# Retention scores taken two rounds earlier, in the preceding token tile's last attention unit

## The chip, the cores and the metric

The kernel runs on one core of one Trainium2 chip. The metric is the device time of one execution in microseconds (us), the median of several runs. The engines are named as in the profile: PE (TensorE, matrix products; PEld its weight loads), DVE (VectorE), ACT (ScalarE), POOL (GpSimd) and SP (SyncE, which here issues the DMAs). Each engine works through its own instructions in the order in which the program lists them, and waits at an instruction until the semaphores named there have been reached.

## What is computed

Two layers of a streaming encoder over 2048 tokens of width 1024. Each layer normalises its input, projects it by `w_in` to eight sections, runs two groups of heads side by side, gates them and projects back by `w_out`:

```python
def hybrid_layer(x, norm_gain, w_in, w_out, rel_bias, cos, sin):
    hn = rms_norm(x, norm_gain)
    aq, ak, av, ag, rq, rk, rv, rg = jnp.split(hn @ w_in, cuts, axis=-1)
    ya = chunked_rel_attention(aq, ak, av, rel_bias)
    yr = chunkwise_retention(rq, rk, rv, cos, sin)
    y = jnp.concatenate([ya * silu(ag), yr * silu(rg)], axis=-1)
    return x + y @ w_out
```

The attention (8 heads of 64) sees a chunk of 64 tokens and the 8 chunks before it. The change concerns the other half, the retention (4 heads of 128). In its chunkwise form, with rotated q and k:

```python
    att = jnp.einsum("bnihd,bnjhd->bnhij", qc, kc) * intra_decay[None, None]
    o_intra = jnp.einsum("bnhij,bnjhe->bnihe", att, vc)
    kv = jnp.einsum("bnjhd,hj,bnjhe->bnhde", kc, k_decay, vc)
    # state is carried over the chunks: state = state * chunk_decay + kv
    o_inter = jnp.einsum("bnihd,hi,bnhde->bnihe", qc, q_decay, states)
    o = rms_norm(o_intra + o_inter)
```

## The kernel before

**Tiling.** The kernel loops over layers l, four head groups s (two attention heads and one retention head each), and four token blocks n of 512 tokens. A block has four token tiles a of 128 tokens; t = 4n + a. All large products are done in two or three terms of f16 halves, so that they keep f32's accuracy: a value is split in an upper half (ACT) and a rest (DVE).

**Rounds.** The order of the instructions of PE, ACT, DVE and POOL is written by hand (`manual_schedule`); only SP's order is left to a scheduler. `run` (L1140) steps through the dense projections of a block: `dense_T` (L608, transposed sections q, k, rotated rq and rk; 12 steps) and `dense_V` (L738, token-major sections v, rv and gates; 12 steps). A step is 8 matmuls of 128x512, a third of one dense product, and is called a round here. After each step, `run` first calls `tick` (L598), which issues the pieces that were put off by `later(k, ...)` (L595) k rounds ago, then takes one step of the attention of the *preceding* block, then pulls some background work (weight preparation, for the first pass also the tables and the normalisation of later tokens, `norms_from_input`, L1154).

**Attention.** `attention` (L778) has 8 units per block, three rounds each: unit (a, hx) for head hx of token tile a. In its first round a unit finishes an older unit's product with v (`flow`, then `pv`, L815, which reads the transposed probabilities pT at L820 to L822) and takes its own scores (`qk`, L785: PE at L800 and L801 into the PSUM tile S, then bias and maximum on DVE at L804, exponential on ACT at L807, halves on ACT and POOL at L809 and L810, and one round later a DMA transpose to pT at L812). Of the two units of a token tile, the one with hx = 0 is called even and the other odd.

**Retention.** The generator `retention` (L866) has two steps per token tile. The first takes the scores r1 (three matmuls of rotated halves, at L856 in the helper `products`), and puts off the multiplication with the decay mask (DVE, L875) by one round, the upper half of dT (ACT, `upper_of`, L860) by two, its rest (DVE, `rest_of`, L864) by three. The second step takes r2: dT with rv, the rotated q with the state's halves sh, and the products of the token-major keys kt with rv for the state; the state's update follows put off in the same way (L896, and `upper_of` and `rest_of` again for sh), and so do the sum of squares, the root on POOL and the gated result (L908 to L913). All four r and o tiles at a time share the PSUM pool `psR` (4 banks); dT is a single buffer.

Counted in rounds from a token tile's first, the scores are taken in round 0, just behind the even unit's attention scores, and r2 in round 5:

```python
            u = qk(a, hx)
            if i % 2 == 0 and not slow:
                next(ret, None)
            yield
            yield
            if i % 2 == 1 or slow:
                next(ret, None)
```

In the first block of all (`slow`) the scores are taken two rounds later, in round 2.

**The rotated keys.** In `dense_T`, `swap` (L664) turns the section's product with the tables in steps put off over several rounds. For rk the low half (`lower`, L676, DVE) is issued in round 19 of the block's 24, and the transpose kt to token-major form (`tokens`, L683, a DMA on SP's queue) in round 23.

Of the kernel before, what the change touches and what calls it, by code (L numbers as in the profile page):

```python
# [18 lines left out]
P = 128  # L19
# [8 lines left out]
def hybrid_trunk(ctx: ExitStack, tc: tile.TileContext, x, pos, gain, gcol, w_in, w_out, rel, fgain,  # L28
# [746 lines left out]
            yield  # L775


    def attention(l, s, n, g, st, prev):  # L778
        units = []
        for a in range(4):  # L780
            for hx in range(2):
                units.append((a, hx))
        ya = {}

        def qk(a, hx):  # L785

            u = St()
            u.a, u.hx = a, hx
            u.nm = f"{l}_{s}_{n}_{a}_{hx}"
            u.nb = nb = min(5, 4 * n + a + 1)  # L790
            u.w = w = nb * P
            u.kts = [(st if t // 4 == n else prev, t % 4) for t in range(4 * n + a + 1 - nb, 4 * n + a + 1)]
            S = psS.tile([P, 1024], F32, tag="S", name=f"S{u.nm}")
            cs = slice(a * P, (a + 1) * P)
            cuts = sorted({0, nb} | {j for j in range(nb) if u.kts[j] == (st, 0) or j == 4})
            for j0, j1 in zip(cuts, cuts[1:]):
                q_, a_ = u.kts[j0]
                k_ = q_.k[:, hx, a_ * P:(a_ + j1 - j0) * P]
                o = S[:, j0 * P:j1 * P]
                pe.matmul(o, st.q[:, hx, 0, cs], k_, start=True, stop=False)  # L800
                pe.matmul(o, st.q[:, hx, 1, cs], k_, start=False, stop=True)  # L801
            v = b2.tile([P, 640], F32, tag="sc", name=f"sc{u.nm}")[:, 0:w]
            m = b2.tile([P, 1], F32, tag="mq", name=f"mq{u.nm}")
            dve.tensor_tensor_reduce(out=v, in0=S[:, 0:w], in1=g.bias[hx][:, 640 - w:640], scale=1.0, scalar=-3.0e38,  # L804
                                     op0=ALU.add, op1=ALU.max, accum_out=m)
            dve.tensor_scalar(m, m, g.nc[:, 0:1], LN_PSC, op0=ALU.mult, op1=ALU.add)  # L806
            act.activation(v, v, AF.Exp, bias=m[:, 0:1], scale=g.c[:, 0:1])  # L807
            pq = b2.tile([P, 1280], F16, tag="pq", name=f"pq{u.nm}")
            act.activation(pq[:, 0:w], v, AF.Copy)  # L809
            pool.tensor_tensor(pq[:, w:2 * w], v, pq[:, 0:w], op=ALU.subtract)  # L810
            u.p = b2.tile([P, 10, P], F16, tag="pT", name=f"pT{u.nm}")[:, 0:2 * nb, :]
            later(1, lambda: sp.dma_start_transpose(out=u.p, in_=pq[:, 0:2 * w]))  # L812
            return u

        def pv(u):  # L815
            t = 4 * n + u.a
            o = psR.tile([P, 512], F32, tag="small", name=f"o{u.nm}")
            for b, (q_, a_) in enumerate(u.kts):
                v_ = q_.v[:, a_, u.hx, :]
                pe.matmul(o[:, 0:65], u.p[:, b, :], v_[:, 0:65], start=(b == 0), stop=False)  # L820
                pe.matmul(o[:, 0:64], u.p[:, b, :], v_[:, 65:129], start=False, stop=False)  # L821
                pe.matmul(o[:, 0:65], u.p[:, u.nb + b, :], v_[:, 0:65], start=False, stop=(b == u.nb - 1))  # L822

            def out_():
                rl = b2.tile([P, 1], F32, tag="rl", name=f"rl{u.nm}")
                dve.reciprocal(rl, o[:, 64:65])
                dve.tensor_tensor(rl, rl, g.ka, op=ALU.mult)
                if u.hx == 0:
                    ya[u.a] = b2.tile([P, P], F32, tag="ya", name=f"ya{u.nm}")
                y = ya[u.a]  # L830
                vs = slice(u.hx * 64, u.hx * 64 + 64)
                dve.scalar_tensor_tensor(out=y[:, vs], in0=o[:, 0:64], scalar=rl[:, 0:1], in1=st.g[u.a][:, vs],
                                         op0=ALU.mult, op1=ALU.mult)
                if u.hx == 1:
                    sp.dma_start(y_d[t][:, s * P:(s + 1) * P], y)

            later(1, out_)

        ret = retention(l, s, n, g, st)
        slow = (l, s, n) == (0, 0, 0)  # L840
        for i, (a, hx) in enumerate(units):
            flow(1)
            u = qk(a, hx)
            if i % 2 == 0 and not slow:
                next(ret, None)
            yield
            yield
            if i % 2 == 1 or slow:
                next(ret, None)
            pipe.append(lambda u=u: pv(u))  # L850
            yield


    def products(out_, pairs):
        for i, (w_, m_) in enumerate(pairs):
            pe.matmul(out_, w_, m_, start=(i == 0), stop=(i + 1 == len(pairs)))  # L856
# [5 lines left out]
    def rest_of(dst, src):  # L862

        dve.scalar_tensor_tensor(out=dst[:, 1], in0=dst[:, 0], scalar=-2.0 ** 11, in1=src, op0=ALU.mult, op1=ALU.add)  # L864

    def retention(l, s, n, g, st):  # L866
        for a in range(4):
            t = 4 * n + a
            nm = f"{l}_{s}_{t}"
            cs = slice(a * P, (a + 1) * P)  # L870
            last = t == NT - 1
            r1 = psR.tile([P, 512], F32, tag="small", name=f"r1{nm}")
            products(r1[:, 0:P], [(st.rk[:, i, cs], st.rq[:, j, cs]) for i, j in ((0, 0), (0, 1), (1, 0))])
            dT = b1.tile([P, 2, P], F16, tag="dT", name=f"dT{nm}")
            later(1, lambda r1=r1: dve.tensor_tensor(r1[:, P:2 * P], r1[:, 0:P], g.msk, op=ALU.mult))  # L875
            later(2, lambda dT=dT, r1=r1: upper_of(dT, r1[:, P:2 * P]))
            later(3, lambda dT=dT, r1=r1: rest_of(dT, r1[:, P:2 * P]))
            yield
            r2 = psR.tile([P, 512], F32, tag="small", name=f"r2{nm}")
            rv = st.rv[a]  # L880
            terms = [(dT[:, 0], rv[:, 0]), (dT[:, 0], rv[:, 1])]
# [477 lines left out]
    for l in range(DEPTH):  # L1359
        gO = [Grp(), Grp()]  # L1360
        go = Grp()
        for s in range(NSW):
            g = grp(l, s)
            for n in range(NS):
                first = (l, s, n) == (0, 0, 0)
                if not first:
                    st = St()
                    states[l, s, n] = st
                    dT = dense_T(l, s, n, g, st)
                else:  # L1370
                    st = st0
                if n == 0 and not first:
                    bs, bt = bias_scratch(l, s), bias_tiles(l, s, g)
                    later(1, lambda bs=bs: next(bs))
                    for k in (4, 8, 17, 21):
                        later(k, lambda bt=bt: next(bt))
                if (l, s) == (0, 0) and 0 < n < NS - 1:
                    if n == 1:
                        push(t1, TAB_STEPS - 10)
                    push(norms_from_input(range(4 * n + 4, 4 * n + 8), late[0:4] if n == 1 else None,  # L1380
                                          tables(n + 1, [xs0[n + 1][:, i * 256:(i + 1) * 256] for i in range(4)])), 21)
                if (l, s, n) == (0, 1, 1):
                    for l_ in range(1, DEPTH):
                        gr = gain_scale(l_)
                        later(2, lambda gr=gr: next(gr))
                        later(10, lambda gr=gr: next(gr))
                        later(18, lambda gr=gr: next(gr))
                if n == (NS - 1 if (l, s) == (0, 0) else 1):
                    if s + 1 < NSW:
                        push(prep_T(l, s + 1, grp(l, s + 1)), 25)  # L1390
                    else:
                        push(prep_O(l, 0, gO[0], go), 9)
                if n == NS - 1 and s == 1 and l + 1 < DEPTH:
                    gain_load(l + 1)
                if not first:
                    run(dT, att, 10 if n == 0 else 14 if (l, s, n) == (0, 0, NS - 1) else 22 if (l, s) == (0, 0) else 24)
                if n == NS - 1 and s == NSW - 1:
                    us = []
                    push(wout_first(l, go, us), 10)
                if n == 2 and s == 2:  # L1400
                    push(prep_Omax(l, go), 13)
                if n == NS - 1:
                    if s + 1 < NSW:
                        push(prep_V(l, s + 1, grp(l, s + 1)), 23)
                    else:
                        push(prep_O(l, 1, gO[1], go), 9)
                run(dense_V(l, s, n, g, st), att, 24 if n == NS - 1 and s < NSW - 1 else 12)
                if first:
                    sp_order.__exit__(None, None, None)
                if att[0] is not None:  # L1410
                    drain(att[0])
                att = [attention(l, s, n, g, st, states.get((l, s, n - 1)))]
        pull(1000)
        if l + 1 == DEPTH:
            ring["fg"] = b3.tile([P, D], F32, tag="wh", name="fg")
# [81 lines left out]
```

## Time and profile before

| | |
|---|---|
| median of 3 runs | 2116.13 us (2115.45 to 2116.34) |
| span of the profiled execution | 2120.7 us, 4.6 us above that median |
| PE busy | 95% of the span |
| DVE busy | 63% |
| ACT busy | 54% |
| POOL busy | 20% |

The profile is of one execution. A time of a row is in us from the start of the span, durations of single instructions in ns where the row says min/median/max. In a table of waits a row reads: engine, what it writes, line, then what ended the wait, then the total, how often and the longest. A line such as L856 is that of a helper, so the names of the tiles tell the use: `r<-rot,rot` are the retention's scores, `r<-rv,dT` the products that read them. In the slices of the page the first two of 40 (the start-up) show the lowest share of PE, 0.6 and 0.7; after them it is 0.8 or more in each.

### The profile page before, as it was taken

To read this page: it belongs to the slowest core of one execution; us is meant where nothing else is said; L and a number is where in the kernel's file an instruction comes from. 1 tells how busy PE (TensorE), PEld (TensorE's weight loads), DVE (VectorE), ACT (ScalarE), POOL (GpSimd) and SP (SyncE) were. 2 spreads that over 40 slices of the span, in tenths; PEclk is the share of its full clock that TensorE was granted. 3 is DMA by queue.
4 is the path that set the end of the run, shared out by engine and by line. 5 is a ranking of instruction groups with operands and counts; after the bars stand their busy time and mean duration, and the time that the engine had idled before them with its cause. 6 is when DMAs were issued, how large, how long until landed. Compare 5 with 4: busy or idle time off the path is not lost.

```text
span 2120.7 us, 39351 instructions
## 1 busy us (share of the span) xinstructions
PE 2014.2 (95%) x14014; PEld 1052.9 (50%) x14014; DVE 1341.8 (63%) x4031; ACT 1136.9 (54%) x2522; POOL 432.8 (20%) x509
## 2 busy tenths in 40 slices
PE   6788999999999999988999999999999999998998
PEld 4334455555555555444444555555555555554543
DVE  7667666666656666566654666566666566666643
ACT  7455565556565554554544546554655665445432
POOL 1112221222122212221000222222222222222200
PEclk9989999999999999999999999999999999999999
DMA  8757675557476765689865556655666866648864
GB/s 247 173 111 162 138 157 119 115 110 156 109 166 133 157 164 100 120 189 254 219 179 123 119 100 135 130 119 100 140 129 123 172 152 157 124 101 176 217 193 127
DMA packets 645702, 313.63 MB, mean 148 GB/s; under 512 B 459233, under 2 KB 602081, under 8 KB 645505
## 3 DMA queue, kind: packets, MB, share of 16 engines
q1 hardware_dynamic: 645504, 311.12, 66.4%
q8 instruction: 109, 1.79, 0.4%
q14 instruction: 89, 0.72, 0.1%
HBM read 123.26 MB, written 41.98 MB: 78 GB/s over the span
## 4 chain that ended last, share of the span: by engine, by line
PE 50%; DMA 8%; DVE 5%; ACT 5%; issue 1%; SPq 1%; POOL 0%; POOLq 0%; DVEq 0%; ACTq 0%
PE dT L731 16%; PE dV L752 15%; PE dO L1093 12%; DMA pT<-pq 3%; PE r L856 2%; PE S L800 2%; PE S L801 2%; DVE sc L804 1%; DMA toep<-rel_d 1%; DMA swp<-rot 1%; PE o L820 1%; ACT pq L809 1%; PE o L821 1%; PE o L822 1%; ACT sc L807 1%
## 5 line engine op out<-in xcount | busy, mean ns | idle before, releaser
L807 ACT ACTIVATE sc<-sc,mq,cT 128x640 f32<-128x640 f32 (+4 forms) x256 | 218.4, 853 | 657.3 <-DVE mq L806 341.5
L810 POOL TENSOR_TENSOR pq<-sc,pq 128x640 f16<-128x640 f32 (+4 forms) x256 | 322.6, 1260 | 1201.7 <-ACT pq L809 610.3
L731 PE MATMUL dT<-hTh,whT 128*128 128x512 f16 x1008 | 350.2, 383 | 13.4 <-DMA hTh<-hTl 9.8
L752 PE MATMUL dV<-whV,hTh 128*128 128x512 f16 x1024 | 355.3, 383 | 4.1 <-DVE gt L770 4.1
L752 PE MATMUL dV<-wlV,hTh 128*128 128x512 f16 x1024 | 353.8, 381 | 0.0
L752 PE MATMUL dV<-whV,hTl 128*128 128x512 f16 x1024 | 353.7, 381 | 0.0
L731 PE MATMUL dT<-hTh,wlT 128*128 128x512 f16 x1008 | 347.0, 379 | 0.0
L731 PE MATMUL dT<-hTl,whT 128*128 128x512 f16 x1008 | 346.8, 379 | 0.0
L752 PEld LDWEIGHTS <-hTh 128*128 128x128 f16 x2048 | 197.5, 99 | 222.9 <-issue 8.2
L731 PEld LDWEIGHTS <-whT 128*128 128x128 f16 x2016 | 192.9, 98 | 225.8 <-issue 23.1
L804 DVE CUSTOM_DVE_ANT_0 sc<-S,bias 128x640 f32<-128x640 f32 (+4 forms) x256 | 188.6, 737 | 79.9 <-PE S L801 69.0
L1093 PE MATMUL dO<-whO,yhy 128*128 128x512 f16 x512 | 195.0, 381 | 1.1 <-DMA yhy<-rhy 1.1
L1093 PE MATMUL dO<-whO,yly 128*128 128x512 f16 x512 | 194.8, 381 | 1.1 <-DMA yly<-rly 1.1
L1093 PE MATMUL dO<-wlO,yhy 128*128 128x512 f16 x512 | 194.6, 380 | 0.0
L809 ACT ACTIVATE pq<-sc 128x640 f16<-128x640 f32 (+4 forms) x256 | 171.5, 670 | 12.5 <-DMA pT<-pq 4.6
L1093 PEld LDWEIGHTS <-yhy 128*128 128x128 f16 x1024 | 100.0, 98 | 116.7 <-DMA yhy<-rhy 1.9
L752 PEld LDWEIGHTS <-hTl 128*128 128x128 f16 x1024 | 99.5, 98 | 110.5 <-issue 2.6
L731 PEld LDWEIGHTS <-wlT 128*128 128x128 f16 x1008 | 97.6, 98 | 109.0 <-issue 1.8
L800 PE MATMUL S<-k,q 128*128 128x128 f16 (+3 forms) x592 | 143.7, 269 | 5.7 <-DVE mq L804 5.6
L820 PE MATMUL o<-v,pT 128*128 128x65 f16 x1120 | 130.2, 194 | 14.6 <-DMA pT<-pq 14.6
L820 PEld LDWEIGHTS <-pT 128*128 128x128 f16 x1120 | 105.6, 97 | 52.5 <-DMA pT<-pq 24.4
L801 PE MATMUL S<-k,q 128*128 128x128 f16 (+3 forms) x592 | 131.2, 270 | 0.0
(350 smaller groups left out, 3354.4 us busy)
## 6 DMA issues: line engine op xcount, KB each, us to landing
q<-qq SPq DMA_DIRECT2D x128, 128.0 KB, 2.5
yyy<-y_d SPq DMA_DIRECT2D x32, 512.0 KB, 4.6
stT<-in_w_in_dram SPq DMA_DIRECT2D x27, 512.0 KB, 5.0
stV<-in_w_in_dram SPq DMA_DIRECT2D x26, 512.0 KB, 4.5
k<-kk SPq DMA_DIRECT2D x128, 64.0 KB, 2.1
swp<-rot SPq DMA_DIRECT2D x64, 128.0 KB, 2.6
tabc<-tab SPq DMA_DIRECT2D x32, 256.0 KB, 2.7
tabs<-tab SPq DMA_DIRECT2D x32, 256.0 KB, 2.8
```

Of the source, the lines that this page charges most:

```text
L731: pe.matmul(ps, w_[:, j, kt, :], h_[:, kt, :], start=(m == 0), stop=(m == 23))
L752: pe.matmul(ps, h_[:, kt, a * P:(a + 1) * P], w_[:, kt, :], start=(m == 0), stop=(m == 23))
L800: pe.matmul(o, st.q[:, hx, 0, cs], k_, start=True, stop=False)
L801: pe.matmul(o, st.q[:, hx, 1, cs], k_, start=False, stop=True)
L804: dve.tensor_tensor_reduce(out=v, in0=S[:, 0:w], in1=g.bias[hx][:, 640 - w:640], scale=1.0, scalar=-3.0e38, op0=ALU.add, op1=ALU.max, accu ...
L807: act.activation(v, v, AF.Exp, bias=m[:, 0:1], scale=g.c[:, 0:1])
L809: act.activation(pq[:, 0:w], v, AF.Copy)
L810: pool.tensor_tensor(pq[:, w:2 * w], v, pq[:, 0:w], op=ALU.subtract)
L820: pe.matmul(o[:, 0:65], u.p[:, b, :], v_[:, 0:65], start=(b == 0), stop=False)
L821: pe.matmul(o[:, 0:64], u.p[:, b, :], v_[:, 65:129], start=False, stop=False)
L856: pe.matmul(out_, w_, m_, start=(i == 0), stop=(i + 1 == len(pairs)))
L1093: pe.matmul(ps, h_[:, kt, :], w_[:, kt, :], start=(m == 0), stop=(m == 23))
```

## The change

The scores of a token tile move out of `retention` into a function of their own, `decayed`. In the odd unit of token tile a, one round after its attention scores, `attention` now calls `decayed` for token tile a + 1; in the last unit of a block for the first token tile of the next block (`nxt`), whose state object is therefore made earlier. Counted from the token tile's first round the scores so stand in round -2, mask, upper half and rest in rounds -1, 0 and 1. `retention` keeps the second step, r2, in round 5. The first block of all takes its first tile's scores in round 2 as before. The first block of the second layer, which has no attention ahead of it, takes them by a `later(11, ...)` in its own dense steps.

```diff
+            yield
+            if hx == 1:
+                if a < 3:
+                    decayed(l, s, n, g, st, a + 1)
+                elif nxt is not None:
+                    decayed(*nxt, 0)
+            yield
+            if hx == 1:
                 next(ret, None)
-            yield
-            yield
-            if i % 2 == 1 or slow:
-                next(ret, None)
+            elif a == 0 and (l, s, n) == (0, 0, 0):
+                decayed(l, s, n, g, st, 0)
...
+    def decayed(l, s, n, g, st, a):
+        nm = f"{l}_{s}_{4 * n + a}"
+        cs = slice(a * P, (a + 1) * P)
+        r1 = psR.tile([P, 512], F32, tag="small", name=f"r1{nm}")
+        products(r1[:, 0:P], [(st.rk[:, i, cs], st.rq[:, j, cs]) for i, j in ((0, 0), (0, 1), (1, 0))])
+
+        def upper():
+            st.dT = b1.tile([P, 2, P], F16, tag="dT", name=f"dT{nm}")
+            upper_of(st.dT, r1[:, P:2 * P])
+
+        later(1, lambda: dve.tensor_tensor(r1[:, P:2 * P], r1[:, 0:P], g.msk, op=ALU.mult))
+        later(2, upper)
+        later(3, lambda: rest_of(st.dT, r1[:, P:2 * P]))
...
-            r1 = psR.tile([P, 512], F32, tag="small", name=f"r1{nm}")
-            products(r1[:, 0:P], [(st.rk[:, i, cs], st.rq[:, j, cs]) for i, j in ((0, 0), (0, 1), (1, 0))])
-            dT = b1.tile([P, 2, P], F16, tag="dT", name=f"dT{nm}")
-            later(1, lambda r1=r1: dve.tensor_tensor(r1[:, P:2 * P], r1[:, 0:P], g.msk, op=ALU.mult))
-            later(2, lambda dT=dT, r1=r1: upper_of(dT, r1[:, P:2 * P]))
-            later(3, lambda dT=dT, r1=r1: rest_of(dT, r1[:, P:2 * P]))
-            yield
+            dT = st.dT
...
+                if (n, s) == (0, 0) and not first:
+                    later(11, lambda n=n, g=g, st=st: decayed(l, s, n, g, st, 0))
```

The instructions of each engine stay the same in number. In the built programs' order, PE's score products, DVE's masks and rests and ACT's upper halves of dT move. In SP's queue, which a scheduler orders, some twenty DMAs change places with a neighbour; among them the transpose kt of the second block, which now stands ahead of the last lower rows hTl of the third block's normalised tokens, and the loads of the next decay mask.

More of the change, by code (lines that the diff above doesn't have):

```diff
@@ L775, in dense_V, with attention @@
             yield
-    def attention(l, s, n, g, st, prev):
+    def attention(l, s, n, g, st, prev, nxt):
         units = []
@@ L839, in attention @@
         ret = retention(l, s, n, g, st)
-        slow = (l, s, n) == (0, 0, 0)
         for i, (a, hx) in enumerate(units):
@@ L843, in attention @@
             u = qk(a, hx)
-            if i % 2 == 0 and not slow:
+            yield
[6 more added lines that the diff above has]
+            if hx == 1:
                 next(ret, None)
-            yield
-            yield
-            if i % 2 == 1 or slow:
-                next(ret, None)
+            elif a == 0 and (l, s, n) == (0, 0, 0):
+                decayed(l, s, n, g, st, 0)
             pipe.append(lambda u=u: pv(u))
@@ L1366, in hybrid_trunk @@
                 if not first:
-                    st = St()
-                    states[l, s, n] = st
+                    st = states.setdefault((l, s, n), St())
                     dT = dense_T(l, s, n, g, st)
@@ L1411, in hybrid_trunk @@
                     drain(att[0])
-                att = [attention(l, s, n, g, st, states.get((l, s, n - 1)))]
+                m = n + 1 if n + 1 < NS else 0
+                nxt = (l, s + (m == 0), m)
+                if nxt[1] < NSW:
+                    nxt += (grp(*nxt[:2]), states.setdefault(nxt, St()))
+                else:
+                    nxt = None
+                att = [attention(l, s, n, g, st, states.get((l, s, n - 1)), nxt)]
         pull(1000)
```

## Prediction

> **What bounds the kernel now.** I read the page first, then the table of who waited for whom, cut by engine and by window, then the timeline at the places that it points to.
>
> ```profile
> span 2120.7 us, 39351 instructions
> PE 2014.2 (95%) x14014; PEld 1052.9 (50%) x14014; DVE 1341.8 (63%) x4031; ACT 1136.9 (54%) x2522; POOL 432.8 (20%) x509
> ```
>
> TensorE (PE) is busy for 95% of the span, so a change that leaves its instructions alone can only win idle time of PE: 2120.7 - 2014.2 = 106.5 us. The sums below are made in this profiled execution, whose span is 4.6 us (0.2%) above the median of the runs, 2116.1 us. I carry the difference over to the median.
>
> What PE waited for stands in the table of waits (total us, times, longest):
>
> ```profile
> PE r L856 <- DVE dT L864: 20.5, 16, 5.1
> PE o L820 <- DMA pT<-pq: 14.6, 13, 2.4
> PE r L856 <- ACT dT L860: 10.2, 6, 2.9
> ...
> PE r L856 <- DVE sh L864: 2.9, 3, 1.7
> ```
>
> The largest item of PE's idle time is the one that the change goes for. The products at L856 that read dT (the decayed scores in two halves, upper from ACT, rest from DVE) wait 20.5 + 10.2 = 30.7 us in 22 places. That is 1.4% of the span, and the ceiling of what dT alone can give back. The other rows matter too: the attention's transposed probabilities pT (14.6 us) and the state's halves sh (2.9 us) come through the same engines, and are what PE would meet next.
>
> **The change part by part.** Nothing is added or removed. Per token tile one mask product, one upper half and one rest move (127 of the 128 of each, in the order of instructions of the built programs), with the three matmuls ahead of them:
>
> ```profile
> L856 PE MATMUL r<-rot,rot x384: 219/219/314, 85.8 to 1977.5; 128*128 128x128 f16 x192
> L875 DVE TENSOR_TENSOR r<-r,msk x128: 286/290/300, 87.9 to 1980.7; 128x128 f32<-128x128 f32 x128
> L860 ACT ACTIVATE dT<-r x128: 253/259/277, 90.7 to 1983.4; 128x128 f16<-128x128 f32 x128
> L864 DVE SCALAR_TENSOR_TENSOR dT<-dT,r x128: 272/278/289, 91.0 to 1985.2; 128x128 f16<-128x128 f16 x128
> ```
>
> Before, with 6 rounds to a token tile, the scores stand in round 0, mask in 1, upper in 2, rest in 3, the reading products in 5. After, they stand in rounds -2, -1, 0, 1, and the products still in 5. PE's work is the same: the three matmuls stood behind the attention scores and now stand alone behind a third of a dense product; I cost that at nothing, between -0.1 us and +0.1 us per token tile (half of the 219 ns of one matmul), and take the middle. PSUM: the built program gives each r1 the bank of the r1 before it, read last by rest, three rounds earlier; no new wait there unless DVE is more than three rounds late.
>
> So dT's slack grows from two rounds to four. Its longest wait is 5.1 us, in the first layer's first pass, where the old order of the very first tile left no slack at all. I expect the dT waits to go. The question is what is late next. I split the 30.7 us by place.
>
> *First pass, 85 to 215 us.* The waits of PE in this window:
>
> ```profile
> PE r L856 <- DVE dT L864: 9.9, 4, 5.1
> PE r L856 <- ACT dT L860: 6.6, 4, 2.9
> PE dT L731 <- DMA hTh<-rhn: 3.6, 1, 3.6
> ```
>
> 16.5 us of dT waits are here. But here DVE and ACT also normalise the next tiles' tokens, and the dense products of a tile (L731) begin when the transposed rows hTh have landed. The second tile's start at 145.24 us and the SP queue and landing of its last rows:
>
> ```profile
> 140.41 2.08 SPq L236 DMA_TRANSPOSE hTh<-rhn  x1
> ...
> DMA to landing us min/median/max: 4.1/4.1/4.1
> ...
> 145.24 1.89 PE L731 MATMUL dT<-hTh,whT 128*128 128x512 f16 x8
> ```
>
> hTh lands at 140.41 + 4.1 = 144.5 us, 0.7 us before PE uses it; at the next such start, 210 us, PE waits for it already (3.6 us above). PE can gain only what the DVE and ACT work ahead of those transposes gains. How much of that work waits for PE?
>
> ```profile
> DVE sc L804 <- PE S L801: 5.1, 3, 3.0
> ```
>
> Only 5.1 us, the longest right behind the 5.1 us stall of PE. Against it stands a move in SP's queue: in the built order the transpose kt of the second tile now stands ahead of the last lower rows hTl, and it waits for products of PE. One such issue costs 1.2 to 1.3 us:
>
> ```profile
> L683 SPq DMA_TRANSPOSE kt<-rot x32: 1231/1349/2368, 85.9 to 1934.7; - x32
> ```
>
> Bounds for this part: -1.3 us (nothing caught up, the transpose in the way) to +16.5 us. I take 5.1 - 1.2 = **3.9 us**, since the hTh row says that PE is held to the DVE chain.
>
> *The rest of the run.* The dT waits from 215 to 960 us, and from 960 us on:
>
> ```profile
> PE r L856 <- DVE dT L864: 6.3, 7, 1.7
> PE r L856 <- ACT dT L860: 1.8, 1, 1.8
> ...
> PE r L856 <- DVE dT L864: 4.3, 5, 1.5
> PE r L856 <- ACT dT L860: 1.8, 1, 1.8
> ```
>
> 14.2 us. Of these 2.6 + 1.0 = 3.6 stand where each layer ends (870 to 980 and 1900 to 1990 us), and there PE waits for pT right behind them:
>
> ```profile
> PE o L820 <- DMA pT<-pq: 5.6, 4, 2.1
> ...
> PE r L856 <- DVE dT L864: 2.6, 2, 1.7
> ...
> PE o L820 <- DMA pT<-pq: 1.2, 2, 0.9
> PE r L856 <- DVE dT L864: 1.0, 1, 1.0
> ```
>
> I count those 3.6 as lost to pT. The other 10.6 us hold two twin places (636 and 1667 us, 2.2 us each). There the new position of the scores meets a wait of its own. They read the low half of the rotated keys, which DVE finishes in the stretch below; PE would stand at the new place at 632.3, where the next dense matmul now starts:
>
> ```profile
> 632.28 0.38 PE L752 MATMUL dV<-whV,hTl 128*128 128x512 f16 x1
> ...
> 632.68 0.68 DVE L676 TENSOR_TENSOR rot<-raw,rot 128x512 f16<-128x512 f32 x1
> ...
> 635.93 0.28 PE L856 MATMUL r<-rv,dT 128*128 128x128 f16 x2 [1.76 <-ACT dT L860]
> ```
>
> The scores wait 632.68 + 0.68 - 632.28 = 1.1 us, half of the 2.2 us that were won. So these two places keep 1.1 us each of 2.2, and 10.6 - 2.2 = 8.4 us remain. Of a won stall, PE keeps as much as the next pT has in hand. An example, the stall of 1.51 us at 730.65:
>
> ```profile
> 730.65 0.23 PE L856 MATMUL r<-rv,dT 128*128 128x128 f16 x1 [1.51 <-DVE dT L864]
> ...
> 734.93 1.34 SPq L812 DMA_TRANSPOSE pT<-pq  x1
> ...
> DMA to landing us min/median/max: 3.4/3.4/3.4
> ...
> 738.97 0.19 PE L820 MATMUL o<-v,pT 128*128 128x65 f16 x1
> ```
>
> pT lands at 734.93 + 3.4 = 738.3, used at 738.97: 0.7 us in hand, so 0.7 of 1.51 is kept, 44%. With that share: 8.4 x 0.44 = **3.7 us** (between 0 and 14.2).
>
> *Displacement.* Mask and upper now stand ahead of the next even unit's bias-and-maximum (DVE) and exponential (ACT), which they stood behind. The odd units have the same work ahead of them as before. Each of 128 even units can lose up to 0.29 + 0.26 = 0.55 us of pT's time. PE's weight loads waited for pT 22 times; ACT waited for DVE ahead of the exponential 145 times in 256:
>
> ```profile
> PEld L820 <- DMA pT<-pq: 24.4, 22, 2.9
> ...
> ACT sc L807 <- DVE mq L806: 341.5, 145, 5.9
> ```
>
> So upper mostly hides in ACT's idle time, and mask costs only where DVE is behind and the unit even. About 11 of the 22 waits would be of even units; a third of them at 0.29 us makes **1.0 us** lost (bounds 0 and 22 x 0.55 = 12.1 us).
>
> Sum: 3.9 + 3.7 - 1.0 = 6.6 us. 2116.1 - 6.6 = **2109.5 us**.
>
> *The clock.* After the 5.07 us stall PE is slow:
>
> ```profile
> 110.43 0.29 PE L856 MATMUL r<-rv,dT 128*128 128x128 f16 x1 [5.07 <-DVE dT L864]
> ...
> 110.83 3.12 PE L752 MATMUL dV<-whV,hTh 128*128 128x512 f16 x8
> ...
> 85.00:145.00 60.00, 47.51 (x264) 22.71 (x263) 40.71 (x116) 33.11 (x71) 10.44 (x15) 0.89 0.59 118
> 145.00:211.00 66.00, 55.92 (x408) 29.32 (x406) 46.84 (x129) 36.85 (x78) 16.30 (x18) 0.96 0.71 152
> ```
>
> Eight matmuls take 3.12 us there and 1.89 us at 145.24, 1.23 us more. At granted clocks of 0.89 and 0.96 the two windows lose up to 47.5 x 0.11 + 55.9 x 0.04 = 7.4 us of PE time. I add nothing for it, since PE is not what sets the end of these windows; it belongs to the first rival.
>
> The Trainium skill, "TensorE: Matmul & The Clock Gate", Part 1, says that PE runs at half rate after an idle window of about 3.4 us and until it has been busy for as long. The rows above agree. The rule speaks against the change at one point: if the short dT stalls of the first pass are gathered into one longer wait for hTh, the matmuls behind that wait start cold, at two starts 2 x 1.23 = 2.5 us, an estimate; the sum would then be 2112.0 us.
>
> **Rivals.**
>
> 1. *Everything is kept* (chance 0.19). The DVE chain follows PE, nothing else is late: 30.7 us and the clock's 7.4 us come back, 2078.0 us; halfway cases lie up to 2103. For it: four rounds of slack against a longest wait of 5.1 us. Against it: the hTh start 0.7 us behind its landing.
> 2. *All is swallowed* (0.28): PE stands at hTh, sh and pT for as long as it stood at dT. 2112 to 2120, middle 2116. For it: pT waits behind the dT waits at both layer ends.
> 3. *Slower* (0.15): mask and upper ahead of the even units push back pT. The 22 pT waits grow by 0.55 us each, 12.1 us, against the 7.6 us won above: 2120.6; with half of those won, 2124.4. It decides from 7.6 / 0.55 = 14 lengthened waits on.
>
> That the change does not do what it says I leave out: the built orders show dT's instructions earlier on ACT and DVE.
>
> **How the numbers follow.** The forecast, 2103 to 2112 us with 2109.5 as its value, has 0.38, the rivals 0.19, 0.28 and 0.15. Faster by over 0.2% (4.2 us, about what a measurement of this kernel tells from no change): 0.38 + 0.19 = 0.57; within it 0.28; slower 0.15. The range of 8 in 10 leaves out the far half of the first rival and most of the third: 2090 to 2121 us.
>
> **What would show it.** In the changed profile the dT rows of PE's waits should fall from 30.7 us below 3 us. If hTh is the pin, its wait at about 205 us grows above 3.6 us, and one appears near 141 us. If pT is what is late next, its 14.6 us grow by some 5 us. A new row "r L856 <- DVE rot L676" of about 1 us in two places shows the keys' wait. The granted clock of the first pass stays below 1. I am wrong if the dT waits stay, if the first pass ends more than 8 us earlier, or if pT's waits grow by more than 8 us.

## The result, and the profile after

The changed kernel takes 2094.49 us (median of 4 runs, 2092.45 to 2094.89) beside 2115.79 us for the kernel before, a ratio of 0.9897 (95% interval 0.9883 to 0.9911). A second measurement (e9 below) gave 2092.76 beside 2113.55 us, 0.9901 (0.9886 to 0.9916). The gain is 21 us; the forecast was 6.6 us.

The head of the page of the changed kernel, the span and the engines' busy time:

```profile
span 2092.8 us, 39599 instructions
PE 2004.4 (96%) x14014; PEld 1049.4 (50%) x14014; DVE 1343.8 (64%) x4031; ACT 1141.3 (55%) x2522; POOL 432.9 (21%) x509
```

The profiled execution of before that the prediction used was a long one, some 6 us above the median of its kernel (a span is about 1.9 us shorter than the time of the same execution). For differences I use a second trace of the same kernel (e1), whose execution took 2117.85 us, 3.3 us above the median of its own runs:

```profile
span 2116.0 us, 39351 instructions
PE 2013.4 (95%) x14014; PEld 1052.1 (50%) x14014; DVE 1341.2 (63%) x4031; ACT 1137.1 (54%) x2522; POOL 433.8 (20%) x509
```

The spans differ by 23.2 us, 2 us more than the medians. PE's busy time falls by 2013.4 - 2004.4 = 9.0 us, though it runs the same 14014 matmuls; the other 14.2 us are time in which PE was not busy. So the gain has two parts, and the prediction counted only the second. What PE waits for, in the changed kernel (line 860 is the helper `products`, line 868 `rest_of`):

```profile
PE dV L752 <- DVE gt L770: 12.8, 6, 4.9
PE o L820 <- DMA pT<-pq: 9.7, 11, 2.2
...
PE r L860 <- DVE sh L868: 2.4, 3, 1.9
PE r L860 <- DVE dT L868: 2.4, 2, 1.3
...
PE r L860 <- DVE rot L676: 0.2, 1, 0.2
```

The 30.7 us of waits of the products for dT are gone. The 2.4 us that still name dT are no products but the scores themselves, in two places (see the timeline further on). pT's waits did not grow by some 5 us, as the prediction had it for the case that pT is late next: they are at 9.7 us, after 14.6 in the trace that the prediction used and 12.1 in e1. New at the head is gt, the last of the V rests on DVE (L770). Most of that stands in the first pass, 85 to 215 us:

```profile
PE dV L752 <- DVE gt L770: 10.3, 4, 4.9
PE dT L731 <- DMA hTh<-rhn: 2.8, 1, 2.8
PE dT L731 <- issue: 2.2, 1, 2.2
```

In the kernel before, this stretch had 16.5 us of dT waits and 3.6 us of hTh. So in the first pass PE does stand elsewhere for most of the time won, mainly at gt. The 2.2 us whose end the last row puts down to "issue" end at 140.13 us, right behind the landing of hTh (issued at 136.18, 3.9 us to landing), so they too are a wait for hTh, which has 5.0 us in place of 3.6. The stretches 85 to 145 and 145 to 215 us (columns as in the prediction, the granted clock third from the end):

```profile
85.00:145.00 60.00, 50.44 (x305) 24.64 (x304) 43.58 (x130) 35.01 (x75) 10.98 (x15) 0.97 0.64 130
145.00:215.00 70.00, 59.31 (x414) 30.81 (x413) 47.63 (x133) 39.25 (x83) 17.95 (x19) 0.93 0.73 151
```

In the first 60 us PE now runs 305 matmuls in place of 264, at a clock of 0.97 in place of 0.89 (308 at 0.94 in e9).

Where along the run does the gain arise? I set the starts of the same dense matmul side by side, e1 against after. The 769th of them starts at 228.7 and 221.2 us: 7.5 us won by the end of the first pass, 3.4 of idle time and 4.1 of busy time. The other 15.7 us come later, 10.8 idle and 4.9 busy, nearly all of it in some ten places; the largest are the end of the first layer (4.2 us), the second of the prediction's twin places (3.9) and the first blocks of two head groups in the second layer (2.9 and 1.8). Most stretches between them take the same time to within 0.02 us. One pair of traces is a small sample: with the second trace of the changed kernel (e9, span 2090.4 us, PE busy 2006.5 us) the split is 6.9 us busy and 18.7 us idle.

### The profile page after: what moved, and what is told of

It reads as the page before. It is cut to its first block, busy times and chain, and to the rows that moved or that the text cites. A ratio compares the mean times of both kernels' runs of the same rounds, so it can differ in the third digit from the quotient of the medians.

```text
span 2092.8 us, 39599 instructions
## 1 busy us (share of the span) xinstructions
PE 2004.4 (96%) x14014; PEld 1049.4 (50%) x14014; DVE 1343.8 (64%) x4031; ACT 1141.3 (55%) x2522; POOL 432.9 (21%) x509
## 4 chain that ended last, share of the span: by engine, by line
PE 55%; DMA 7%; DVE 5%; ACT 3%; issue 1%; SPq 1%; POOL 0%; POOLq 0%; DVEq 0%; ACTq 0%
PE dT L731 18%; PE dV L752 15%; PE dO L1105 12%; DMA pT<-pq 2%; PE r L860 2%; PE S L801 2%; PE S L800 2%; PE o L820 1%; PE o L821 1%; PE o L822 1%; DVE sc L804 1%; DMA swp<-rot 1%; DMA yhy<-rhy 1%; ACT sc L807 1%; ACT pq L809 1%
## 5 line engine op out<-in xcount | busy, mean ns | idle before, releaser
L807 ACT ACTIVATE sc<-sc,mq,cT 128x640 f32<-128x640 f32 (+4 forms) x256 | 218.5, 853 | 558.1 <-DVE mq L806 413.7
L800 PE MATMUL S<-k,q 128*128 128x128 f16 (+3 forms) x592 | 143.1, 268 | 7.9 <-DVE mq L804 7.9
```

## The experiments

Twelve runs. Rounds are counted as in the section on the kernel before: scores 0, mask 1, upper 2, rest 3 before; -2, -1, 0, 1 after; the reading products in 5. "Lateness" below is the mean time from a unit's first score product (L800) to its exponential (L807), over the 128 even and the 128 odd units of a trace. The kernel before ran beside each group of experiments, with medians of 2113.5 to 2114.0 us; its single runs lay up to 8 us away from them. The ratios on record and the quotients of the medians differ by up to 0.0011, some 2 us; where it matters I give the gain by both.

**e1: the kernel before, once more.** No edit.

> The kernel before, unchanged, profiled a second time. Theory A (the trace of before that the prediction used is a typical one): span within 1 us of 2120.7 us, dT waits of PE within 2 us of 30.7 us and pT waits within 2 us of 14.6 us. Theory B (that trace was a slow sample, so that some of the 27.9 us between the two spans is not the change's): a span of 2111 to 2116 us, with pT or other DMA waits lower by several us. Time against before: ratio 1.000 within 0.001 by both.

2114.52 us, ratio 0.9998 (0.9990 to 1.0007). The dT waits are 16.0 + 11.7 = 27.7 us, 3.0 below the first trace, pT's 12.1 us, 2.5 below, and the span is 2116.0 us: theory B. So the dT waits are no accident of one execution, but the trace that the prediction used was a long execution with larger waits.

**e2: no wait for dT at all, nothing moved.** The three products read a constant in place of dT, so the own-chunk term is left out; mask, upper and rest are still done.

```diff
-            terms = [(dT[:, 0], rv[:, 0]), (dT[:, 0], rv[:, 1])]
+            dfix = ident.bitcast(F16).rearrange("p (h c) -> p h c", h=2)
+            terms = [(dfix[:, 0], rv[:, 0]), (dfix[:, 0], rv[:, 1])]
...
-            products(r2[:, 0:P], terms + [(dT[:, 1], rv[:, 2])])
+            products(r2[:, 0:P], terms + [(dfix[:, 1], rv[:, 2])])
```

> The kernel before with every instruction in its old place, but the reading products read a constant tile in place of dT (the scores, mask, upper half and rest are still computed, and not used; so the retention's own-chunk term is left out). PE so cannot wait for dT, and nothing is displaced. Theory A (the gain is the removed dT waits and nothing else): 2094 to 2097 us, like the changed kernel. Theory B (moving mask and upper half ahead of the even units has a price, as the prediction said, of 1 to 12 us): 2083 to 2093 us, faster than the changed kernel. Theory C (the new order also helps pT by itself): 2098 to 2106 us, slower than the changed kernel.

2102.47 us, ratio 0.9934 (0.9920 to 0.9947): 14 us below before by the ratio, 12 by the medians, and 8 to 10 above the changed kernel. Its largest waits:

```profile
PE o L820 <- DMA pT<-pq: 13.3, 13, 2.1
PE dV L752 <- DVE gt L770: 12.5, 8, 4.9
```

Taking away the dT waits alone does not make the whole gain, at least in this measurement: of some 28 to 31 us of waits it returns 12 to 14. PE's busy time is 2006.2 us here, 7.2 below e1, though no instruction has moved: it falls with the stalls.

**e3 and e4: the change in two parts.** e3 makes the change everywhere but in the first block of all, e4 there alone. The edit against the changed kernel in e3:

```diff
+            slow = (l, s, n) == (0, 0, 0)
...
-                    decayed(l, s, n, g, st, a + 1)
+                    if not slow:
+                        decayed(l, s, n, g, st, a + 1)
...
-            elif a == 0 and (l, s, n) == (0, 0, 0):
-                decayed(l, s, n, g, st, 0)
+            elif slow:
+                decayed(l, s, n, g, st, a)
```

e4 is the mirror of it: `decayed` two rounds sooner only for `slow`, else in the even unit's first round.

> The change everywhere but in the first block of the first layer, whose scores stay where they were (no slack between rest and the reading products). Theory A (the first pass is held by the normalised rows hTh, so its dT stalls are worth little): within 3 us of the changed kernel, 2094 to 2098 us. Theory B (the stalls of the first block, some 12 us of waits and the slow clock behind them, come back in full): 2104 to 2110 us. The gain at 226 us, 5.9 us in the trace, says 2098 to 2101 us if all of it belongs to the first block.

> The change only in the first block of the first layer; all other blocks take their scores in round 0 as before. Theory A: 2112 to 2116 us (0 to 4 us gained). Theory B: 2104 to 2108 us. The sum of this gain and that of the kernel with the change everywhere else should be the whole, 21 us, if the parts do not act on one another.

e3: 2099.05 us, ratio 0.9923 (0.9909 to 0.9937), that is 16.3 us won by the ratio (15.0 by the medians). e4: 2112.02 us, 0.9986 (0.9975 to 0.9996), 3.0 us won (2.0 by the medians), with the same longest gt wait in its first pass, 4.9 us. The sum, 17.0 to 19.3, is the whole gain but for 2 to 4 us. So the first block returns about what the prediction gave to the first pass (3.9 us), and the mis-sized part is the rest of the run. (The stretch up to 215 us reaches into the second block, and e4 still has 4.0 us of dT waits there.)

**e5: PE's move alone.** The scores stay two rounds sooner; mask, upper and rest go back to rounds 1, 2 and 3.

```diff
-        later(1, lambda: dve.tensor_tensor(r1[:, P:2 * P], r1[:, 0:P], g.msk, op=ALU.mult))
-        later(2, upper)
-        later(3, lambda: rest_of(st.dT, r1[:, P:2 * P]))
+        d = 2 if (l, s, n) != (0, 0, 0) else 4 if a > 0 else 0
+        later(1 + d, lambda: dve.tensor_tensor(r1[:, P:2 * P], r1[:, 0:P], g.msk, op=ALU.mult))
+        later(2 + d, upper)
+        later(3 + d, lambda: rest_of(st.dT, r1[:, P:2 * P]))
```

> TensorE issues the scores two rounds sooner, as in the changed kernel, but the mask, the upper half and the rest of dT stay in the rounds where they were before (1, 2 and 3). If the time is won because dT is finished sooner or because mask and rest leave their old places on VectorE, nearly all of the 21 us is gone again: 2110 to 2117 us, with the dT waits back at 16 to 30 us. If it is the place of the scores on TensorE that counts, it stays at 2093 to 2098 us.

2114.74 us, ratio 1.0006 (0.9995 to 1.0018): nothing is left. The dT waits are back, and there is a wait that no other order so far had:

```profile
PE r L860 <- DVE dT L868: 14.0, 10, 4.5
...
PE r L860 <- ACT dT L864: 6.2, 3, 2.7
PE msT L323 <- DVE dT L868: 5.8, 10, 0.8
...
PE r L860 <- DVE ya L832: 4.0, 2, 2.2
```

msT is a small PSUM tile of the same four-buffer pool as r1. With the scores early and the rest late, r1 holds its buffer five rounds in place of three, and others of the pool wait for it.

**e6: e2's constant in the changed kernel** (own-chunk term left out again).

> The changed kernel, with products that read a constant in place of dT (the own-chunk term is left out, as in e2). No wait for dT can exist here, as in e2, so the two differ only in where scores, mask, upper and rest stand. If the excess over the dT waits is the worth of the new places, 2092 to 2096 us (6 to 10 us below e2's 2102.5). If e2 lost something of its own by the constant operand, this one is at 2100 to 2104 us too.

2098.38 us, ratio 0.9928 (0.9914 to 0.9942), between the two expectations. It was run again as e10, beside the changed kernel as e9:

> The changed kernel once more, beside e10 on the same chip. The waits that can be counted on TensorE explain a gain of some 14 to 18 us, its faster clock the rest: TensorE's busy time should again be 5 to 10 us below the 2013.4 and 2014.2 us of the two traces of the kernel before, and the time 2093 to 2098 us. If the low busy time of the first trace was chance, it is at 2010 us or more and the time at 2098 to 2102 us.

> e6 once more (products read a constant, the own-chunk term is left out), now beside the changed kernel itself. If the constant costs nothing, it is within 2 us of e9, and then the new places of mask and rest on VectorE are worth nothing that can be measured, since e2 gave the same as e6. If it is 3 to 5 us above e9, the constant operand costs that much in itself, and e2 understated what the dT waits are worth.

e9: 2092.76 us, 0.9901 (0.9886 to 0.9916), PE busy 2006.5 us. e10: 2093.06 us, 0.9902 (0.9888 to 0.9916). So the constant costs nothing in itself, the low busy time of the first trace was no chance, and the changed kernel has nothing left to win at dT. e6 and e10 are the same kernel, 5 us apart in two measurements on two chips (4 and 9), while the kernel before has 2113.66 and 2113.55 us there: between measurements, less than some 5 us is not told apart. What the new order is worth on its own, e2 against e6 and e10, is therefore only known as 4 to 9 us by the times, 1 to 7 by the ratios; the intervals of e2 and e6 overlap.

**e7: e2 with the rest of dT one round later**, round 4 in place of 3.

```diff
-            later(3, lambda dT=dT, r1=r1: rest_of(dT, r1[:, P:2 * P]))
+            later(4, lambda dT=dT, r1=r1: rest_of(dT, r1[:, P:2 * P]))
```

> e2 with one thing changed: the rest of dT stands in round 4 in place of round 3, so it no longer stands right ahead of the odd unit's bias-and-maximum on VectorE. If that one place is the cause of the further gain, 2095 to 2098 us with pT's waits below e2's 13.3 us. If the gain is from the mask and the scores, 2101 to 2104 us, as e2.

2098.71 us, ratio 0.9931 (0.9918 to 0.9944), the same as e2 within the intervals: by time alone this does not decide. The lateness of the odd units falls from 3.48 us (e2) to 3.19 us, about the 0.28 us of one rest; but pT's waits hardly move (12.4 us), and with the buffer of r1 held for a round longer, PE waits 8.3 us for this rest in 7 places, which e2 did not have.

**e8: the changed kernel with only the rest back in round 3.**

```diff
-        later(3, lambda: rest_of(st.dT, r1[:, P:2 * P]))
+        later(3 if (l, s, n, a) == (0, 0, 0, 0) else 5, lambda: rest_of(st.dT, r1[:, P:2 * P]))
```

> The changed kernel with only the rest of dT put back into round 3 (scores, mask and upper stay sooner). The upper half can no longer be late, the rest can: the waits of the products for VectorE's dT come back, 10 to 20 us, and rest stands ahead of the odd unit's bias-and-maximum again. If both count, 2104 to 2112 us. If it was the upper half on ScalarE and the mask that won the time, 2094 to 2099 us.

2107.10 us, ratio 0.9965 (0.9951 to 0.9979): two thirds of the gain are gone. The dT waits and the buffer's are back:

```profile
PE r L860 <- DVE dT L868: 11.6, 8, 4.1
...
PE msT L323 <- DVE dT L868: 5.0, 10, 0.8
...
PE r L860 <- DVE ya L832: 3.3, 3, 1.3
```

**e11: mask, upper and rest one round later than in the changed kernel** (0, 1, 2).

```diff
+        d = 0 if (l, s, n, a) == (0, 0, 0, 0) else 1
-        later(1, lambda: dve.tensor_tensor(r1[:, P:2 * P], r1[:, 0:P], g.msk, op=ALU.mult))
-        later(2, upper)
-        later(3, lambda: rest_of(st.dT, r1[:, P:2 * P]))
+        later(1 + d, lambda: dve.tensor_tensor(r1[:, P:2 * P], r1[:, 0:P], g.msk, op=ALU.mult))
+        later(2 + d, upper)
+        later(3 + d, lambda: rest_of(st.dT, r1[:, P:2 * P]))
```

> The changed kernel with mask, upper and rest each one round later (0, 1 and 2 in place of -1, 0 and 1; the very first token tile as in the changed kernel). Between the changed kernel and e5. If the gain is slack for dT, most of it is there after one round: 2095 to 2100 us, with dT waits of 3 to 8 us. If the place of mask and rest counts, the mask stands behind the even unit's bias-and-maximum again and it can come out below the changed kernel, 2090 to 2093 us.

2108.64 us (12 runs, 2102.76 to 2115.43), ratio 0.9973 (0.9963 to 0.9983). Neither expectation held. Few dT waits are left, but 15 to 16 us of the gain are gone. Two suspects: the buffer of r1, held four rounds here, and the rounds themselves. So the last run moves the whole chain, with the buffer held for three rounds as ever.

**e12: everything one round sooner, not two** (scores -1, mask 0, upper 1, rest 2).

```diff
             yield
-            if hx == 1:
-                if a < 3:
-                    decayed(l, s, n, g, st, a + 1)
-                elif nxt is not None:
-                    decayed(*nxt, 0)
             yield
             if hx == 1:
                 next(ret, None)
+                if a < 3:
+                    decayed(l, s, n, g, st, a + 1)
+                elif nxt is not None:
+                    decayed(*nxt, 0)
```

> The whole chain of a token tile one round sooner than in the kernel before, in place of two: scores in round -1 (behind the products of the preceding tile), mask 0, upper 1, rest 2; so mask, upper and rest stand in the rounds that they have in e11, but the PSUM buffer of the scores is held for three rounds, as in the kernel before and in the changed one, and not for four. If e11 lost its gain by the buffer held for a round longer, this kernel keeps most of it: 2094 to 2099 us, without the waits for VectorE's ya and dT at scores and at msT. If it is the rounds of mask and rest that decide, or the second round of slack, it is at 2104 to 2109 us, as e11.

2110.64 us, ratio 0.9990 (0.9976 to 1.0003): no gain to speak of. And yet the dT waits are all but gone. The head of its page and its waits, first those of pT, then sh, msT, dT:

```profile
span 2108.9 us, 39389 instructions
PE 2015.5 (96%) x14014; PEld 1051.6 (50%) x14014; DVE 1335.5 (63%) x4031; ACT 1133.9 (54%) x2522; POOL 430.6 (20%) x509
```

```profile
PE o L820 <- DMA pT<-pq: 14.1, 13, 3.2
...
PE r L859 <- DVE sh L867: 5.7, 5, 2.3
...
PE msT L323 <- DVE mbT L316: 5.2, 7, 2.0
...
PE r L859 <- DVE dT L867: 1.0, 6, 0.2
```

The same rows of e9, the changed kernel:

```profile
PE o L820 <- DMA pT<-pq: 9.0, 11, 1.9
...
PE msT L323 <- DVE mbT L316: 2.9, 3, 1.9
...
PE r L860 <- DVE sh L868: 2.4, 3, 2.0
```

pT, sh and msT all come through DVE, and PE waits 25.0 us for them together in e12 against 14.3 us in e9. One trace is thin ground for such a sum: e6 and e10, one kernel, have 20.2 and 12.7 us. e12 against e9 is the cleanest pair of the study: the products hardly wait for dT (1.0 us in six places in e12, nothing in e9, where the 2.3 us that name dT are the scores, at the buffer of r1, in the two twin places), and both hold the buffer for three rounds. They ran in two measurements, with the kernel before at 2113.51 and 2113.55 us beside them. The span differs by 18.5 us, 9.0 of it PE's busy time (2015.5 against 2006.5), and all of it behind the first pass: the same dense matmul that starts at 221.2 us in the changed kernel's first trace starts at 219.4 us in e12 and 220.2 in e9. What differs is where scores, mask, upper and rest stand, each one round later; the rows below are of mask and rest in DVE's queue. The queue around the same even unit, in the second layer's third head group, in e12 (mask is line 879, rest of dT 867, bias and maximum 804):

```profile
1609.02 0.28 DVE L832 SCALAR_TENSOR_TENSOR ya<-o,rl,gt 128x64 f32<-128x64 f32 x1
1611.21 0.69 DVE L648 SCALAR_TENSOR_TENSOR kk<-dT,kk 128x512 f16<-128x512 f32 x1 [1.91 <-ACT kk L645]
1611.82 0.28 DVE L907 SCALAR_TENSOR_TENSOR state<-r,state 128x128 f32<-128x128 f32 x1
1612.02 0.29 DVE L879 TENSOR_TENSOR r<-r,msk 128x128 f32<-128x128 f32 x1
1612.22 0.81 DVE L804 CUSTOM_DVE_ANT_0 sc<-S,bias 128x640 f32<-128x640 f32 x1
```

And in e9 (mask is line 880):

```profile
1596.92 0.28 DVE L832 SCALAR_TENSOR_TENSOR ya<-o,rl,gt 128x64 f32<-128x64 f32 x1
1597.12 0.29 DVE L880 TENSOR_TENSOR r<-r,msk 128x128 f32<-128x128 f32 x1
1599.12 0.69 DVE L648 SCALAR_TENSOR_TENSOR kk<-dT,kk 128x512 f16<-128x512 f32 x1 [1.70 <-ACT kk L645]
1599.73 0.28 DVE L908 SCALAR_TENSOR_TENSOR state<-r,state 128x128 f32<-128x128 f32 x1
1600.07 0.82 DVE L804 CUSTOM_DVE_ANT_0 sc<-S,bias 128x640 f32<-128x640 f32 x1
```

Both DVEs stand idle for 1.7 to 1.9 us until ACT has written kk. In the changed kernel the mask stands ahead of that wait and is done in it, for nothing. In e12 the same mask stands behind the wait and right ahead of the bias-and-maximum, and pushes it back by 0.20 us. The rest changes its place in the same way, from ahead of the wait for sh to behind it, further on in the queue. This unit's lateness is 2.53 us in e12 and 1.92 in e9: the mask is a third of the difference. The remainder is there before the mask, since ACT's kk comes later against PE's scores; whether earlier pushes add up to that is not shown. Over the whole run the lateness of even and odd units is 2.83 and 3.42 us before (e1; 2.90 and 3.48 in the first trace), 2.90 and 3.37 in the changed kernel (e9), 3.06 and 3.50 in e12. But mean lateness does not order the runs: e2, 8 us faster than e12, has 3.00 and 3.48, and e5, with no gain, 2.77 and 3.41. The Trainium skill, "PSUM — Partial Sum Buffer", section "Engine vs sequencer instructions", calls the queues of ScalarE, VectorE and GpSimdE strict FIFO; the two timelines agree: what stands behind a waiting instruction is not taken ahead of it.

The buffer is so acquitted as the cause of e11, since e12 does not have its waits and is no faster. It is shown that the round decides. That it decides through DVE's queue is argued from these rows and not shown: no run put only the mask or only the rest behind its wait with nothing else changed, and ACT's upper half and PE's scores moved by the same round. e8 did so for the rest, but with the buffer's waits beside it. Of all orders run, the changed kernel's is the fastest; none of the others points to a better one.

## Why the prediction was right in sign and wrong in size

The result is not in the forecast's 2103 to 2112 us but in the band of the first rival, "Everything is kept", whose halfway cases lie up to 2103 us (chance 0.19): 21 us came back of that rival's 30.7 and 7.4.

**"A change that leaves PE's instructions alone can only win idle time of PE"** fell. 9.0 of 23.2 us are busy time. Behind many of the longer stalls PE runs slowly, so a stall that goes takes the slow matmuls behind it along. Of the 7760 matmuls of 128x512, 75 took over 0.5 us in e1 and 46 in the changed kernel (60 in e9, 85 in e12). The two traces of the kernel before show the price at one place, the second twin place. In e1:

```profile
1659.89 0.39 PE L856 MATMUL r<-rv,dT 128*128 128x128 f16 x2 [2.78 <-ACT dT L860]
...
1661.22 3.58 PE L731 MATMUL dT<-hTh,whT 128*128 128x512 f16 x8
```

In the trace that the prediction used, the same eight matmuls behind a shorter stall:

```profile
1666.14 0.29 PE L856 MATMUL r<-rv,dT 128*128 128x128 f16 x2 [1.76 <-ACT dT L860]
...
1667.27 1.89 PE L731 MATMUL dT<-hTh,whT 128*128 128x512 f16 x8
```

The changed kernel still shows the pattern at 129.5 us, behind the longest gt wait, and a few rows later at full speed:

```profile
129.54 0.61 PE L752 MATMUL dV<-whV,hTh 128*128 128x512 f16 x1 [4.88 <-DVE gt L770]
129.94 0.63 PE L752 MATMUL dV<-whV,hTl 128*128 128x512 f16 x1
...
133.63 0.38 PE L752 MATMUL dV<-wlV,hTh 128*128 128x512 f16 x1
```

**The clock, "I add nothing for it"**, is the step that failed by this. The term was put at 0, with up to 7.4 us left to the first rival; it measured 4.1 us in the first pass and 4.9 us behind it (6.9 us in all by the trace of e9, 1.2 of it in the first pass). The reason given, that PE does not set the end of the first pass, did not cover the rest of the run, where the stalls have slow matmuls behind them too.

**First pass, 3.9 us kept of 16.5.** Right in size for the first block: e4 measured 3.0 us (0.9 to 5.3, by its interval). By the traces the pass itself ends 7.5 us earlier (6.1 to 8.5 over the pairs of traces), 3.4 of it idle time, near the 8 us from which the prediction called itself wrong. Right also that PE is held there by DVE's chain, but mainly at another link: hTh's wait at about 205 us did not grow (3.6 us before, 2.8 after), a wait of 2.2 us appeared at 140.1 us as forecast, and the main wait is gt, 10.3 us, which the prediction did not name. The transpose kt in SP's way, 1.2 us, was not tried by itself; in the trace PE shows no wait for the hTl behind it.

**The rest of the run, 3.7 us kept of 14.2.** This is the mis-sized term: e3 measured 16.3 us (13.3 to 19.2; 15.0 by the medians). In the traces 10.8 us of it are idle time and 4.9 us the clock. Two choices failed. The 3.6 us at the layer ends, counted as lost to pT, were for the most part kept: pT's waits there, 5.6 and 1.2 us before, are these after:

```profile
PE o L820 <- DMA pT<-pq: 5.7, 4, 2.2
...
PE o L820 <- DMA pT<-pq: 0.5, 1, 0.5
```

Between the same matmuls at the end of the first layer PE's idle time fell from 13.7 to 9.9 us, by more than the 2.6 us of dT; at the second layer's end PE's waits fell from 6.9 to 6.4 us, by half of the 1.0.

And the share of 44% (0.7 of 1.51 is 46%, which would make the term 3.9 us) came from one stall and took pT's landing as fixed. At that very place, 728 us in the new trace, PE waits 0.54 us for pT, so 0.97 of 1.51 us were kept, 64%. Elsewhere pT came earlier by itself: in the first blocks of two head groups, PE waits 2.17 and 1.56 us for it in e1 and 1.08 us and not at all after. Why it came earlier there was not tried.

**The two twin places** have the forecast's wait at the scores, 1.1 and 1.3 us, but for another reason than the keys alone, and they did not keep 1.1 us each: PE waits 0.73 and 0.55 us more right behind (msO, for DVE's yr), so that 0.35 us are won at each against the trace that the prediction used. The 3.9 us won against e1 at the second are 1.1 us of stall and 2.8 us of the slow matmuls shown above. DVE's queue at the first place, and PE:

```profile
623.67 0.68 DVE L676 TENSOR_TENSOR rot<-raw,rot 128x512 f16<-128x512 f32 x1
624.27 0.28 DVE L868 SCALAR_TENSOR_TENSOR dT<-dT,r 128x128 f16<-128x128 f16 x1
```

```profile
624.60 0.33 PE L860 MATMUL r<-rot,rot 128*128 128x128 f16 x3 [1.09 <-DVE dT L868]
```

The keys' low half is done at 624.35, but the rest of the preceding tile stands right behind it, ends at 624.55, and only then is the PSUM buffer of r1 free. The sentence "no new wait there unless DVE is more than three rounds late" met its exception here.

**Displacement, -1.0 us.** The reason was read off the wrong side. "Mask and upper now stand ahead of the next even unit's work" counted what stands ahead, and not whether DVE waits in between. The mask does stand ahead of the even unit, but a round ahead, where DVE waits for ACT: the even lateness rose by 0.07 us of a possible 0.29, no more than the two traces of before differ. "The odd units have the same work ahead of them as before" was wrong as well: the rest left its place right ahead of the odd unit's bias-and-maximum for one behind the even unit's, and the odd lateness fell by 0.05 us. The forecast displacement is real one round later, in e12: +0.23 us for even units and +0.08 us for odd ones against e1. There nearly the whole gain is gone, as the second rival said; but e2 has nearly as late even units (+0.17) and keeps 12 to 14 us, so the lateness alone does not account for it.

**What would show it.** dT's rows fell as forecast. That pT would be late next, by 5 us more, did not come; in e12 too pT's 14.1 us are no more than the 14.6 and 12.1 of the two traces of before, though 5.1 above e9.

## What to carry to other kernels

When a piece of work is moved in an in-order queue, look at the rows with idle time around the new place: a piece that lands ahead of a wait can be free, and the same piece behind the wait delays the critical instruction that follows (0.20 us in the rows of e12). One round made a difference of 18 us here (e12 against e9); the rows give a direction for it, not its size. Count a stall of PE with the slow matmuls behind it, some 0.4 to 0.6 us of busy time for each us of idle time in this kernel (6.9 to 18.7 and 9.0 to 14.2). A tile that is produced sooner must also be consumed sooner, or its PSUM buffer is held longer and a neighbour of the pool waits (e5, e8).

## What the runs showed of the hardware

A wait of 2.81 us was enough for the slow clock here. In the changed kernel, without another wait in the 5 us ahead of it:

```profile
204.90 3.40 PE L731 MATMUL dT<-hTh,whT 128*128 128x512 f16 x8 [2.81 <-DMA hTh<-rhn]
```

Eight matmuls take 3.40 us, against 1.89 us for the eight at 145.24 in the kernel before. The Trainium skill, "TensorE: Matmul & The Clock Gate", Part 1, puts the idle window at about 3.4 us; the 4.88 us wait above agrees with that, this one is shorter. Nor does the length of one wait decide. In e1 2.17 us were followed by slow matmuls, with no other wait in the 7 us ahead:

```profile
1310.00 0.20 PE L820 MATMUL o<-v,pT 128*128 128x65 f16 x1 [2.17 <-DMA pT<-pq]
...
1311.78 0.63 PE L731 MATMUL dT<-hTh,whT 128*128 128x512 f16 x1
```

In the changed kernel 2.21 us were not:

```profile
140.13 1.89 PE L731 MATMUL dT<-hTh,whT 128*128 128x512 f16 x8 [2.21 <-issue]
```

The second surprise is the scatter: e6 and e10, one kernel, differ by 5 us between two measurements, and a gain of less than that needs runs side by side.
